# Eleven products of a decoder layer computed by token and turned by transposing DMAs

## The chip, the cores and the metric

The kernel runs on one core of a Trainium2 chip. The metric is the time of one execution on the device, in microseconds. A run executes the whole layer once. For a profile, one execution is recorded by the hardware profiler.

## The reference

A hybrid decoder layer for one sequence of 256 tokens, model width 2048, in float32. With `hn = rmsnorm(h)`:

```python
q, k, v, g_ret, xr, yr, g_a, g_b = split(hn @ w_in)      # widths 1024 1024 2048 2048 2048 2048 2048 2048
q, k   = rotary(q, positions), rotary(k, positions) * 128**-0.5
ret    = head_groupnorm(chunkwise_retention(q, k, v))    # 8 heads, chunks of 128 tokens
xr     = causal_dwconv(xr, rnn_conv_w, rnn_conv_b)       # 4 taps along the tokens
hr     = rg_lru(xr, ...)                                 # gates by 16 blocks of 128, scan along the tokens
merged = sigmoid(g_a) * ((silu(g_ret) * ret) @ w_proj_ret) + sigmoid(g_b) * ((gelu(yr) * hr) @ w_proj_rnn)
h      = h + merged @ w_mix_out
h      = h + memory_cross_attention(rmsnorm(h), rmsnorm(mem), ...)   # 256 memory tokens, 4 heads
h      = h + conv_gated_ffn(rmsnorm(h), ...)             # width 5632, conv of 3 taps
out    = rmsnorm(h)
```

The change touches `q`, `k`, `xr` and `yr`: they are the four parts of `hn @ w_in` that are used with features on the partitions (rotation across features, convolution and scan along tokens).

## The kernel before

**Products in two parts.** Every large product is made from float32 numbers split into a high and a low part (`hi` and `lo`, type float32r): high by high, high by low and low by high are summed. Weights come as pieces of 4 x 128 rows by 512 columns (1 MB). A planner's list, `weight_plan`, fixes their order, and `prefetch` keeps two pieces ahead (`AHEAD = 2`): a load on SP's queue into `raw` (six buffers), `hi` by a ScalarE copy (line 286), `lo` by a VectorE subtraction (line 287), three buffers each. One piece is one unit of the loop `units`. A paired product (`pair_products`) computes two column blocks with fewer multiplications; its eleven units are half or full ones, and two of them get their weights by a load that accumulates on GpSimd's queue, after a VectorE addition (line 294).

**Two forms of a product.** `gemm_n` gives rows: tokens on the partitions, 512 features in the free dimension; the activations are the stationary operand and the weights stream, 24 matmuls of 512 columns a unit (lines 362, 363, 369). `gemm_t` gives columns: features on the partitions, 256 tokens in the free dimension; the weights are stationary. It streams high and low activations together (512 columns) through each high weight block and the high activations (256 columns) through each low one, 16 and 16 matmuls a unit (line 351). Its result lies in two PSUM tiles, in halves that `joined` adds (a ScalarE copy, line 544, and a VectorE addition, line 545). `scaled` is `joined` and a multiplication by the token's reciprocal root mean square `rsb2` (line 676).

**A turn by DMA.** In the feed-forward part, all but three of the up products are already made by `gemm_n` and turned: `planes` copies the float32 rows as two planes of 16-bit words (line 757), `turn_planes` issues two transposing DMAs from SP's queue (line 1205), `join_planes` puts the words together again by two ScalarE copies for each pair of feature blocks (line 763), and a multiplication by `rsb2` follows (line 1271). The three that aren't so made use `gemm_t`, as do the first queries.

**The order of work.** The program is one straight line. `later(n, fn)` puts off a piece of work until n + 1 units have gone by. In it stand, among others, the retention (`retain`: scores, values, statistics, head stores), and the recurrence (`recur`: gates by TensorE at line 948, exponentials, scan). The scheduler orders each engine's instructions by the program's order and by what is ready, and fixes that order before the run; buffers come from pools (`big`: 24 of 4 KB a partition, `tmp`: 10 of 2 KB, three PSUM tiles `acc`).

For each of the two groups of four heads the kernel before computes queries by `gemm_t`, values by `gemm_n` or as a pair, keys by `gemm_t`, gates as a pair, and then the retention. `rotated` turns queries and keys by position (lines 720, 722, 726, and the split at 552 and 553). Then come four recurrent blocks; each makes `xr` and `yr` by `gemm_t`, with `scaled`, the convolution (lines 995 and 997) or the gelu (lines 1005 to 1009) right behind it.

Of the kernel before, what the change touches and what calls it, by code (L numbers as in the profile page):

```python
# [29 lines left out]
KC = 4  # L30
# [124 lines left out]
def hybrid_layer(  # L155
# [37 lines left out]
    def tmp(s="t"):  # L193
        return tp.tile([P, 2, S], F32, tag="tmp", name=nm(s))
# [109 lines left out]
    def later(n, fn):  # L304

        pending.append((step[0] + n + 1, fn))
# [403 lines left out]

    def rotated(qs_):

        o = []
        cb = cos[:, None, :].to_broadcast([P, 2, S])
        for pr in range(2):
            q = qs_[pr]
            ta, tb = tmp("ta"), tmp("tb")
            dve.tensor_tensor(out=ta, in0=q, in1=cb, op=ALU.mult)  # L720
            for lo_, hi_ in ((0, 64), (64, 128)):
                dve.tensor_tensor(  # L722
                    out=tb[lo_:hi_], in0=q[64 - lo_ : 128 - lo_],
                    in1=sin[64 - lo_ : 128 - lo_, None, :].to_broadcast([64, 2, S]), op=ALU.mult,
                )
            dve.tensor_add(ta, ta, tb)
            o.append(split_pair(ta))
        return o

    class Kept(list):  # L730
# [9 lines left out]
        def __getitem__(self, i):  # L740
# [9 lines left out]
    def words(t):  # L750

        return t.bitcast(U16).rearrange("p t (w two) -> p t w two", two=2)

    def planes(t, rows, cs=slice(0, BW)):

        for i in range(2):
            act.copy(t[:, :, i, cs], words(rows)[:, :, :, 1 - i])

    def join_planes(d, pr):

        t = tmp("jp")
        for i in range(2):
            ins = act.copy(words(t)[:, :, :, 1 - i], d[:, i, 2 * pr : 2 * pr + 2, :])  # L763
            if i == 0:
                tc.keep_in_program_order(ins)
        return t

    class KeptRows(list):
        def __init__(self, name, wcol=None):
# [112 lines left out]
    for g in range(2):  # L882
        dec = big([P, 4, S], s="dec")
        vs, turned = [], []
        for b, o in enumerate((O_Q, O_K)):
            a = qjoin if g == b == 0 else [joined(t, "q") for t in gemm_t("w_in", 0, xs, NT, o + g * BW)]
            if b == 0:
                sp.dma_start(
                    out=dec,
                    in_=consts[:, C_DEC + g * 4 * S : C_DEC + (g + 1) * 4 * S].rearrange("p (h s) -> p h s", s=S),  # L890
                )
            if g > 0:
                turned.append(rotated(a))
                if b == 0:
                    vs += [split_rows(v, rs0) for v in pair_out("w_in", xs, xs_sums, O_V + 1024)]
            else:
                if b == 1:
                    turned.append(rotated(a))
                v = gemm_n("w_in", 0, xs, NT, O_V + b * BW)
                if b == 0:  # L900
                    turned.append(rotated(a))
                    for i in range(KC):
                        later(i, lambda i=i: sum_x(i))
                vs.append(split_rows(v, rs0))
        qr, kr = turned
# [79 lines left out]
    def recurrent(b):  # L985
        rgw = big([P, 2, 4, P], s="rgw")
        for i, src in enumerate((rg_w_a, rg_w_x)):
            sp.dma_start(out=rgw[:, i], in_=src[0, 4 * b : 4 * b + 4].rearrange("g i j -> i g j"))
        xr = big([P, 4, S], s="xr")
        for pr, a in enumerate(gemm_t("w_in", 0, xs, NT, O_XR + b * BW)):  # L990
            z = scaled(a, "xz")
            for j in range(2):
                t = 4 * b + 2 * pr + j
                y = xr[:, 2 * pr + j, :]
                act.activation(y, z[:, j, :], AF.Identity, scale=p_cw(3, t), bias=p_cb(t))
                for s in range(1, 4):
                    dve.scalar_tensor_tensor(
                        out=y[:, s:S], in0=z[:, j, 0 : S - s], scalar=p_cw(3 - s, t), in1=y[:, s:S],
                        op0=ALU.mult, op1=ALU.add,
                    )  # L1000
        gl = big([P, 4, S], s="gl")
        for pr, a in enumerate(gemm_t("w_in", 0, xs, NT, O_YR + b * BW)):
            y = scaled(a, "yz")
            y2, th = tmp("y2"), tmp("yt")
            act.activation(y2, y, AF.Square)
            dve.tensor_scalar(out=y2, in0=y2, scalar1=0.044715 * K0, scalar2=K0, op0=ALU.mult, op1=ALU.add)
# [175 lines left out]

    qs = KeptRows("qs")

    def row_planes(o):

        t = big([P, 2, 2, BW], U16, s="rp")
        planes(t, o)
        return t

    for b in (0, 2):
        for i in range(KC):
            if b == 0 and i < 2:
# [7 lines left out]
    def turn_planes(rows):  # L1201

        d = big([P, 2, KC, S], U16, s="d")
        for tt in range(2):
            sp.dma_start_transpose(  # L1205
                out=d.rearrange("p a c s -> p (a c) s")[:, :, tt * P : (tt + 1) * P],
                in_=rows[:, tt].rearrange("p a w -> p (a w)"),
            )
        return d

    def turn_key(b, o):
        d = turn_planes(row_planes(o))
# [48 lines left out]
    def up(c0, b, at, then):  # L1261

        if at is None:
            for pr, a in enumerate(gemm_t("ffn_w_up", 0, h2s, NT, c0 + b * BW)):
                then(pr, scaled(a, "uz"))
            return
        d = turn_planes(row_planes(gemm_n("ffn_w_up", 0, h2s, NT, c0 + b * BW)))

        def turned(pr):
            z = join_planes(d, pr)  # L1270
            dve.tensor_tensor(out=z, in0=z, in1=rsb2, op=ALU.mult)
            then(pr, z)

        for pr in range(2):
            later(at[pr], lambda pr=pr: turned(pr))

    def conv(c0, b, pr, z, dst):
        for j in range(2):
# [84 lines left out]
    for part, nb_ in enumerate(FF_PARTS):  # L1363
# [3 lines left out]
        for b in range(b0, b0 + nb_):  # L1367
            gt, vl = big([P, 4, S], s="fg"), big([P, 4, S], s="fv")
            last = b + 1 == b0 + nb_
            up(0, b, (1, 2), lambda pr, z, b=b, gt=gt: conv(0, b, pr, z, gt))  # L1370
            if last:
                later(0, lambda part=part, n=2 if paired else 4: get_rows(part % 2, range(n)))

# [4 lines left out]
            if last and paired:  # L1378
                for pr, a in enumerate(gemm_t("ffn_w_up", 0, h2s, NT, FF + b * BW)):
                    later(1 + 2 * pr, lambda pr=pr, z=scaled(a, "uz"): finish_up(pr, z))  # L1380
            else:
                up(FF, b, None if last else (1, 2), finish_up)
        if final:
            wfin = []
            for i in range(2):
# [51 lines left out]
```

## Time and profile before

| | |
|---|---|
| median of 3 runs | 1984.11 us (1982.38 to 1986.17) |
| the profiled execution | 1986.44 us |
| its span | 1984.6 us, granted TensorE clock 0.998 |
| busy: TensorE, VectorE, ScalarE | 1968.9, 1568.1, 1271.2 us |
| data read and written in device memory | 420.96 MB and 16.78 MB |

The span runs from the first to the last recorded instruction; what the profiled execution has beyond it lies before and after. Busy times of an engine are the union of its instructions. In the lines below, PE is TensorE's matmul, PEld its weight load, DVE is VectorE, ACT ScalarE, POOL GpSimd, SP the sync engine; a "q" behind the name is the engine's instruction queue. `out<-in` are the program's names of the tiles. In a group the two numbers behind the bar are busy microseconds and the mean nanoseconds of one instruction, then the idle time of the engine just before them, with what ended it.

### The profile page before, as it was taken

The page shows a single profiled execution, that of the slowest core. Times are in us where ns is not written, and L with a number is a line of the kernel's source. Part 1 is how long each engine was busy: PE and PEld are TensorE (multiplying, and loading weights), DVE is VectorE, ACT ScalarE, POOL GpSimd, SP SyncE. Part 2 cuts the span into 40 slices and gives each one's busy share as a digit, 9 for nine tenths or more (in the row PEclk, how much of TensorE's full clock was granted, in tenths as well). Part 3 has the DMA queues.
Part 4 walks back from the last instruction along what each step waited for, and adds up shares of the span by engine and source line. Part 5 has one row for each costly group of instructions (what it writes and reads, how often), then busy time and mean ns, then how long its engine had stood idle before and what let it go on. Part 6 is the DMA issues. An engine that isn't in the chain of part 4 may idle for free.

```text
span 1984.6 us, 23752 instructions
## 1 busy us (share of the span) xinstructions
PE 1968.9 (99%) x9368; PEld 1653.5 (83%) x9368; DVE 1568.1 (79%) x1550; ACT 1271.2 (64%) x1315; POOL 43.2 (2%) x52
## 2 busy tenths in 40 slices
PE   9999999999999999999999999999999999999998
PEld 8888888888888888888888888888878888888887
DVE  6988887889986876778888868677797776985775
ACT  6555656768667654566878756567754676646663
POOL 0000000000000000000000000000000000000000
PEclk9999999999999999999999999999999999999999
DMA  9675674655887775778998838767778567786671
GB/s 365 235 256 149 234 260 164 217 205 143 274 256 220 254 254 179 249 264 241 287 249 231 288 113 233 266 222 221 214 239 284 196 224 239 224 279 232 212 245 63
DMA packets 142239, 455.54 MB, mean 230 GB/s; under 512 B 73520, under 2 KB 78256, under 8 KB 94384
## 3 DMA queue, kind: packets, MB, share of 16 engines
q1 hardware_dynamic: 134848, 409.46, 58.7%
q0 software_dynamic: 5760, 41.95, 11.6%
q10 hardware_dynamic: 1520, 2.63, 0.4%
q8 instruction: 73, 1.20, 0.2%
q14 instruction: 38, 0.31, 0.0%
HBM read 420.96 MB, written 16.78 MB: 221 GB/s over the span
## 4 chain that ended last, share of the span: by engine, by line
PE 90%; DVE 4%; issue 2%; DMA 2%; ACT 1%; SPq 0%; POOLq 0%; ACTq 0%; DVEq 0%
PE acc L369 24%; PE acc L362 24%; PE acc L363 24%; PE acc L351 15%; PE sm L518 2%; DVE lo L287 2%; DMA raw<-in_wall 2%; ACT hi L286 1%; PE acc L518 1%; PE sm L948 1%; PE sm L532 1%; DVE raw L294 0%; DVE fv L1283 0%; DVE tb L722 0%; SPq L1205 0%
## 5 line engine op out<-in xcount | busy, mean ns | idle before, releaser
L287 DVE TENSOR_TENSOR lo<-raw,hi 128x2048 fp32r<-128x2048 f32 (+1 forms) x420 | 951.1, 2268 | 283.9 <-ACT hi L286 279.5
L286 ACT CAST hi<-raw 128x2048 fp32r<-128x2048 f32 (+1 forms) x418 | 792.7, 1901 | 511.7 <-PE acc L363 353.7
L362 PE MATMUL acc<-hi,s 128*128 128x512 f32 x1944 | 760.1, 391 | 2.1 <-ACT s L555 2.1
L363 PE MATMUL acc<-hi,s 128*128 128x512 f32 x1944 | 758.0, 390 | 0.4 <-DVE s L556 0.4
L369 PE MATMUL acc<-lo,s 128*128 128x512 f32 x1944 | 485.2, 389 | 0.0
L362 PEld LDWEIGHTS acc<-hi,s 128*128 128x128 f32 x1944 | 365.5, 188 | 78.0 <-ACT s L555 3.3
L363 PEld LDWEIGHTS acc<-hi,s 128*128 128x128 f32 x1944 | 365.7, 188 | 76.2 <-DVE s L556 1.3
L369 PEld LDWEIGHTS acc<-lo,s 128*128 128x128 f32 x1944 | 364.9, 188 | 75.8
L351 PE MATMUL acc<-s,hi 128*128 128x512 f32 x960 | 232.1, 393 | 0.9 <-DVE hi L284 0.9
L351 PEld LDWEIGHTS acc<-s,hi 128*128 128x128 f32 x960 | 178.0, 189 | 36.8 <-issue 1.1
L351 PEld LDWEIGHTS acc<-s,lo 128*128 128x128 f32 x960 | 123.9, 192 | 5.2 <-DVE lo L287 1.1
L351 PE MATMUL acc<-s,lo 128*128 128x256 f32 x960 | 127.2, 284 | 0.5 <-DVE lo L287 0.5
L362 PE MATMUL acc<-hi,ss 128*128 128x512 f32 x320 | 125.8, 393 | 1.1 <-ACT o L454 0.6
L363 PE MATMUL acc<-hi,ss 128*128 128x512 f32 x320 | 124.7, 390 | 0.0
L763 ACT COPY jp<-d 128x512 uint16<-128x512 uint16 x124 | 87.9, 772 | 35.0 <-DMA d<-rp 34.8
L369 PE MATMUL acc<-lo,ss 128*128 128x512 f32 x320 | 85.6, 389 | 0.0
L362 PEld LDWEIGHTS acc<-hi,ss 128*128 128x128 f32 x320 | 60.1, 188 | 15.1 <-ACT o L454 1.5
L369 PEld LDWEIGHTS acc<-lo,ss 128*128 128x128 f32 x320 | 60.1, 188 | 12.6
L363 PEld LDWEIGHTS acc<-hi,ss 128*128 128x128 f32 x320 | 60.1, 188 | 12.1
L267 POOL DMA_DIRECT2D raw<-in_wall x40 | 35.2, 879 | 1543.5 <-DVE lo L287 1047.5
L427 DVE TENSOR_TENSOR nat<-nat,acc 128x512 f32<-128x512 f32 (+1 forms) x49 | 44.0, 910 | 6.0 <-PE acc L369 6.0
L292 DVE TENSOR_TENSOR raw<-raw,raw 128x2048 f32<-128x2048 f32 x20 | 45.8, 2289 | 0.4
(235 smaller groups left out, 1254.8 us busy)
## 6 DMA issues: line engine op xcount, KB each, us to landing
raw<-in_wall SPq DMA_DIRECT2D x333, 1024.0 KB, 5.1
raw<-in_wall POOLq DMA_DIRECT2D x40, 1024.0 KB, 8.2
fkept<-nat SPq DMA_DIRECT2D x12, 512.0 KB, 7.6
nat<-fkept SPq DMA_DIRECT2D x12, 512.0 KB, 4.6
xt<-in_x_t SPq DMA_DIRECT2D x11, 256.0 KB, 8.0
raw<-in_wall SPq DMA_DIRECT2D x5, 512.0 KB, 8.6
nat<-in_x ACTq DMA_DIRECT2D x4, 512.0 KB, 9.8
ret<-hr SPq DMA_DIRECT2D x4, 512.0 KB, 4.7
```

What stands on the lines that cost most here:

```text
L267: pool.dma_start(out=raw, in_=src, accum_op=ALU.add)
L286: act.copy(hi[:, a:b], raw[:, a:b])
L287: dve.tensor_tensor(out=lo[:, a:b], in0=raw[:, a:b], in1=hi[:, a:b].bitcast(F32), op=ALU.subtract)
L292: dve.tensor_tensor(out=to, in0=to, in1=by, op=ALU.add)
L351: pe.matmul(a, part, sx, start=k == 0 and t == 0, stop=k == nk - 1 and t == 0, skip_group_check=True)
L362: pe.matmul(o, h, hi, start=start and kk == 0, stop=False, skip_group_check=True)
L363: pe.matmul(o, l, hi, start=False, stop=False, skip_group_check=True)
L369: pe.matmul(o, h, lo, start=False, stop=stop and kk == KC - 1, skip_group_check=True)
L427: dve.tensor_tensor(out=o, in0=o, in1=i, op=op)
L518: ins = pe.matmul(o, a, b, start=start and i == 0, stop=stop and i == 2, skip_group_check=True)
L532: ins = pe.transpose(t[:, j, tt * P : (tt + 1) * P], rows[:, tt, k + j * P : k + (j + 1) * P], ident)
L763: ins = act.copy(words(t)[:, :, :, 1 - i], d[:, i, 2 * pr : 2 * pr + 2, :])
```

## The change

Eleven products go from `gemm_t` to `gemm_n` with the turn by DMA: keys of the first head group, queries and keys of the second, `xr` and `yr` of the four recurrent blocks. The first queries stay as they are. The helpers of the turn move up in the file, and `gemm_turned` puts them together: product, planes, transposes, and for each of the two pairs of feature blocks a join put off by `at` (and `at + 1`) units, with `then` behind it. `at` is 1 for the first keys and for the recurrent products, 3 where paired products follow. With `shared` (recurrent products) the second of the two plane copies is VectorE's. `by_rs` multiplies by `rsb2`. The feed-forward part uses the same helper with the delays that it had.

```diff
+    def planes(t, rows, cs=slice(0, BW), shared=False):
+        for i in range(2):
+            copy = dve.tensor_copy if i and shared else act.copy
+            copy(t[:, :, i, cs], words(rows)[:, :, :, 1 - i])
...
+    def gemm_turned(w, st, col, at, then, shared=False):
+        d = turn_planes(row_planes(gemm_n(w, 0, st, NT, col), shared))
+        for pr in range(2):
+            later(at + pr, lambda pr=pr: then(pr, join_planes(d, pr)))
+
+    def by_rs(z):
+        dve.tensor_tensor(out=z, in0=z, in1=rsb2, op=ALU.mult)
+        return z
...
-        for b, o in enumerate((O_Q, O_K)):
-            a = qjoin if g == b == 0 else [joined(t, "q") for t in gemm_t("w_in", 0, xs, NT, o + g * BW)]
...
+        def block(o, at, turned=turned):
+            halves_ = []
+            def then(pr, z):
+                halves_.append(z)
+                if pr == 1:
+                    turned.append(rotated(halves_))
+            gemm_turned("w_in", xs, o + g * BW, at, then)
+
+        if g == 0:
+            vs.append(split_rows(gemm_n("w_in", 0, xs, NT, O_V), rs0))
+            turned.append(rotated(qjoin))
+            for i in range(KC):
+                later(i, lambda i=i: sum_x(i))
+            block(O_K, 1)
+            vs.append(split_rows(gemm_n("w_in", 0, xs, NT, O_V + BW), rs0))
+        else:
+            block(O_Q, 3)
+            vs += [split_rows(v, rs0) for v in pair_out("w_in", xs, xs_sums, O_V + 1024)]
+            block(O_K, 3)
         gates = [head_gate(a, big([P, 2, BW], s="gate")) for a in pair_out("w_in", xs, xs_sums, O_G + g * 1024)]
-        retain(g, qr, kr, vs, dec, gates)
+        retain(g, *turned, vs, dec, gates)
...
-        for pr, a in enumerate(gemm_t("w_in", 0, xs, NT, O_XR + b * BW)):
-            z = scaled(a, "xz")
+        def conv_x(pr, z):
+            by_rs(z)
...
+        gemm_turned("w_in", xs, O_XR + b * BW, 1, conv_x, True)
...
-        for pr, a in enumerate(gemm_t("w_in", 0, xs, NT, O_YR + b * BW)):
-            y = scaled(a, "yz")
+        def gelu(pr, y):
+            by_rs(y)
...
+        gemm_turned("w_in", xs, O_YR + b * BW, 1, gelu, True)
         later(0, lambda: recur(b, rgw, xr, gl))
...
-        d = turn_planes(row_planes(gemm_n("ffn_w_up", 0, h2s, NT, c0 + b * BW)))
...
+        gemm_turned("ffn_w_up", h2s, c0 + b * BW, at, lambda pr, z: then(pr, by_rs(z)))
```

More of the change, by code (lines that the diff above doesn't have):

```diff
@@ L748, in __getitem__ @@
             return list.__getitem__(self, i)
[L750 to L766, printed above, removed]
     class KeptRows(list):
@@ L1183, in hybrid_layer @@
     qs = KeptRows("qs")
[L1185 to L1189, printed above, removed]
     for b in (0, 2):
@@ L1199, in hybrid_layer @@
             later(1 + 2 * i, lambda b=b + i, o=o: qs.store(b, row_planes(o)))
[L1201 to L1209, printed above, removed]
     def turn_key(b, o):
@@ L1381, in hybrid_layer @@
             else:
-                up(FF, b, None if last else (1, 2), finish_up)
+                up(FF, b, None if last else 1, finish_up)
         if final:
```

52 lines of the change are left out of this document (26 added, 26 removed).

## The prediction

> **What bounds the kernel now.** I read the page's busy shares first, then TensorE's own waits (engine, tile and line, who it waited for: us in all, times, longest), then the chain of work in order of time, and last the timeline and the windows of the stages that the change touches.
>
> ```profile
> span 1984.6 us, 23752 instructions
> PE 1968.9 (99%) x9368; PEld 1653.5 (83%) x9368; DVE 1568.1 (79%) x1550; ACT 1271.2 (64%) x1315; POOL 43.2 (2%) x52
> ...
> PE acc L362 <- ACT s L555: 2.1, 3, 1.5
> ...
> PE acc L362 <- ACT o L454: 0.6, 2, 0.3
> ...
> PE acc L362 <- DVE o L470: 0.5, 1, 0.5
> ```
>
> TensorE is idle for 1984.6 - 1968.9 = 15.7 us in all. The three waits shown are 3.2 us of it; the last two, 1.1 us together, lie in the paired products of values and gates of the second head group, a part that the change touches. So only TensorE's own work, or new idle time on it, can move the end. VectorE and ScalarE matter only where they come too late for TensorE.
>
> ```profile
> 345.74 38.94 PE acc L351 x224
> 386.41 5.55 PE acc L351 x32
> 393.70 38.94 PE acc L351 x224
> 434.37 5.55 PE acc L351 x32
> ...
> 1281.01 1.81 PE acc L369 x8
> 1286.45 1.81 PE acc L369 x8
> ...
> 1378.93 1.81 PE acc L369 x8
> ```
>
> This is the chain in order of time (start, length, what). Line 351 is the product by feature (`gemm_t`); 224 matmuls are seven weight units of 32, so a unit costs 38.94 / 7 = 5.563 us. Lines 362, 363 and 369 are the product by token (`gemm_n`), 24 matmuls a unit; the closing group of eight recurs every (1378.93 - 1281.01) / 18 = 5.440 us. Both stretches run without a gap.
>
> ```profile
> 450.70 4.00 PE L351 MATMUL acc<-s,lo 128*128 128x256 f32 x32
> 454.53 7.44 PE L351 MATMUL acc<-s,hi 128*128 128x512 f32 x32
> 461.81 3.04 PE L351 MATMUL acc<-s,lo 128*128 128x256 f32 x24
> ```
>
> The timeline of TensorE says why the two differ though both stream 12,288 columns a unit. From start to start, 32 matmuls of 256 columns take 3.83 us (0.1197 each) and 32 of 512 take 7.28 us (0.2275 each). The narrow one costs more than half of the wide one. `gemm_t` has 16 of each a unit, 5.555 us; `gemm_n` has 24 wide ones.
>
> **The change part by part.** Eleven products of four units each (keys of the first head group, queries and keys of the second, four recurrent inputs, four recurrent gates) go from `gemm_t` to `gemm_n`. All of it is on the path: 44 x (5.563 - 5.440) = 5.4 us less of TensorE. No other TensorE instruction is added or removed, since the turn is made by DMA.
>
> Around it the other engines' work changes:
>
> ```profile
> L763 ACT COPY jp<-d 128x512 uint16<-128x512 uint16 x124 | 87.9, 772 | 35.0 <-DMA d<-rp 34.8 <-DMA d<-ret 0.2
> ...
> L757 ACT COPY rp<-acc 128x1024 uint16<-128x1024 uint16 x38 | 36.3, 1007 | 0.0
> ...
> L460 DVE TENSOR_TENSOR o<-o,acc 128x1024 f32<-128x1024 f32 x22 | 26.8, 1218 | 10.5 <-PE acc L369 10.4
> ...
> L544 ACT COPY c<-acc 128x512 f32<-128x512 f32 x30 | 17.2, 579 | 11.5 <-PE acc L351 11.1
> ...
> L722 DVE TENSOR_TENSOR tb<-q,sin 64x512 f32<-64x512 f32 x16 | 11.0, 686 | 0.3
> ...
> L545 DVE TENSOR_TENSOR xz<-acc,c 128x512 f32<-128x512 f32 x8 | 5.4, 679 | 0.0
> ...
> L1006 DVE TENSOR_SCALAR y<-y 128x512 f32<-128x512 f32 x8 | 3.4, 422 | 1.4 <-ACT y L1005 1.4
> ```
>
> These are groups by line and shape (mean ns behind the comma). Each product loses two ScalarE copies of half sums (2 x 0.579) and two VectorE additions (2 x 0.679). It gains two plane copies out of PSUM and four joining copies (4 x 0.772 = 3.09 us, ScalarE). For keys and queries both plane copies are ScalarE's (2 x 1.007): +3.94 us for ScalarE, -1.36 for VectorE. For the eight recurrent products one plane is VectorE's: +2.94 us for ScalarE. VectorE's price for that copy isn't in the trace. Below it lies twice the one-source 512-element row, 0.84 us; above it the 1024-element addition that also reads PSUM, 1.22 us. I take 1.22, since it shares the PSUM source: -0.14 us for VectorE a product. The multiplication by the token scale stays, now at its own place in a shared helper.
>
> The Trainium skill (VectorE: DVE Perf Modes, "The perf-mode tier table" and "Mode 2×_1P") says that a PSUM operand leaves at most the packed double rate and that this needs 16-bit elements at step one; the copy reads every second 16-bit word, so it would run at one element a cycle, an estimate of (120 + 1024) / 0.96 = 1.19 us by that page's cycle table. The sum would be the same; no run here shows it yet.
>
> ```profile
> core 0: us, PE busy (x) PEld busy (x) DVE busy (x) ACT busy (x) POOL busy (x), PEclk, DMA share, GB/s
> 338.46:386.41 47.95, 47.95 (x274) 42.39 (x273) 40.67 (x48) 37.21 (x49) 0.00 (x0) 1.00 0.69 241
> 386.41:434.37 47.96, 47.96 (x274) 42.40 (x273) 39.71 (x46) 32.16 (x40) 0.00 (x0) 1.00 0.55 198
> 469.30:516.80 47.50, 47.50 (x213) 39.48 (x212) 45.58 (x37) 40.31 (x45) 1.75 (x2) 1.00 0.74 217
> 1281.00:1379.00 98.00, 98.00 (x435) 81.12 (x434) 73.52 (x90) 68.82 (x73) 0.00 (x0) 1.00 0.67 214
> ```
>
> In these windows the first two are recurrent blocks (the first still stores heads), the third the paired gate product behind the last block, the fourth the feed-forward part, which already works as the change wants it. A recurrent block loses 8 x 0.123 = 1.0 us on TensorE, so it lasts 47.0. ScalarE goes from 32.16 to 32.16 + 2 x 2.94 = 38.0 us (81%), with head stores 43.1 (92%); VectorE stays at 39.4 (84%). The feed-forward window shows planes, transposes and joins at 70 to 75% load with TensorE at 98.00 of 98.00. So inside the blocks I cost the added work at nothing: the cover is the two units that the casts run ahead, about 11 us.
>
> ```profile
> SPq L265 <- DVE lo L287: 1131.2, 259, 16.9
> ...
> SPq L1205 <- ACT rp L757: 56.1, 14, 5.9
> ...
> ACT hi L286 <- PE acc L351: 43.1, 30, 4.7
> ACT jp L763 <- DMA d<-rp: 34.8, 15, 4.8
> ...
> d<-rp SPq DMA_TRANSPOSE x46, 3.3
> ```
>
> The 22 new transposes go through SP's queue. Behind an SP instruction that waits for the planes (5.9 us at worst so far) stand the weight loads, and behind them the casts. Those loads wait for free buffers anyhow, 1131.2 us in total, and six raw buffers of 5.4 us hold more than 30 us: nothing. A join on ScalarE waits for its transpose (34.8 us in 15 cases, 4.8 the longest); queued behind it are weight casts. ScalarE's waits for TensorE to free a cast buffer (43.1 us by line 351) say that the casts run as far ahead as buffers allow. `gemm_n` also uses the low weights last in a unit, where `gemm_t` has them first in every second one. Nothing, with the price of this cover in the rivals.
>
> Two places have less cover, because paired products have units of half length. Behind the last block:
>
> ```profile
> 487.68 1.92 ACT L286 CAST hi<-raw 128x2048 fp32r<-128x2048 f32 x1
> 489.61 1.28 ACT L963 ACT_TABLE_LOAD   x1
> 490.91 1.06 ACT L963 ACTIVATE tt<-tt 128x1024 f32<-128x1024 f32 x1
> 492.04 1.07 ACT L454 COPY o<-acc 128x512 f32<-128x512 f32 x2
> 493.00 5.55 ACT L286 CAST hi<-raw 128x2048 fp32r<-128x2048 f32 x3
> ...
> 495.39 4.49 DVE L287 TENSOR_TENSOR lo<-raw,hi 128x2048 fp32r<-128x2048 f32 x2
> ...
> 497.28 0.39 PE L362 MATMUL acc<-hi,s 128*128 128x512 f32 x1
> ...
> 500.90 1.98 PE L369 MATMUL acc<-lo,s 128*128 128x512 f32 x8
> ```
>
> ScalarE is full here. The first of three casts ends at 494.9, and TensorE wants it at 497.28: 2.4 us of cover. The last recurrent gates add 1.0 + 3.1 - 0.6 (one of the two half-sum copies already fell before) = 3.5 us ahead of it. So TensorE would wait 1.1 us; VectorE's low cast (4.49 / 2 = 2.25 us, begun at 495.39) isn't wanted until 500.90. I charge +1.1; the bounds are 0 (the scheduler moves the cast ahead) and 3.5 (no cover).
>
> The other place is the second head group's queries and keys. Their joins and the rotation move from the start of a paired product to its fourth and fifth unit. A rotation is ten VectorE operations of about 0.69 us, 6.9 us, and now stands before the short units; its old place becomes free, and the addition that starts the accumulating load comes earlier. Bounds: -1.1 us (the two old waits go) to +6.9 us each (no cover). Casts two units ahead and a 5.4 us unit right behind the short ones lie nearer to the lower end: 0.
>
> Sum: -5.4 + 1.1 = -4.3 us. Against the profiled execution (span 1984.6, time 1986.44, 1.84 outside the span) that is a span of 1980.3. The median of runs, 1984.11, is 2.3 below the profiled time; with the same -4.3 it becomes 1979.8. About 0.2%, 4.0 us, is what a measurement of this kernel can tell from no change, so the forecast lies just beyond it.
>
> **The rivals.**
>
> *Given back in part.* Each of the three paired products costs 1.1 to 1.8 us as in the sum, because every one gets planes and joins: 5.4 - 3 x 1.5 = 0.9 us remain, 1983.2. For it: ScalarE at 40.31 of 47.50 and VectorE at 45.58 in the third window. Against it: casts ahead elsewhere.
>
> *The narrow matmul was not the cost.* If 256 columns cost just their share, nothing is gained but a fixed piece per matmul. With 0.1137 (half of 0.2275) a unit of `gemm_t` would be 16 x 0.3412 = 5.46 us, and 44 x 0.02 = 0.9 us would be left: 1983.2. Against it: 5.563 and 5.440 come from long gapless stretches of this trace. The Trainium skill (VectorE: DVE Perf Modes, "The TRN2 errata") gives a matmul max(60, 6 + columns) cycles of 2.4 GHz, an estimate of 5.20 and 5.18 us for the two units, thus 0.9 us over the 44. The trace disagrees: 0.1197 us where that rule gives 0.109.
>
> *Slower: the rotation lands before the short units.* Three short units need three low casts and one weight addition from VectorE, 4 x 2.3 = 9.2 us in 3 x 2.72 = 8.2; with 6.9 more it is 7.9 behind, against 5.4 us of casts ahead. From 2.7 us of idle TensorE a place, at two places, the gain is gone. With the whole rotation uncovered it is 2 x 6.9 - 5.4 = +8.4 us: 1992.5; with half, +1.5. For it: VectorE's 96% in a paired product. Against: rotation and low casts have different readiness, and the order can be filled.
>
> **How the numbers follow.** Forecast 0.65, of which 0.10 ends less than 4.0 us below; given back 0.13; narrow matmul not the cost 0.05; slower 0.17. Faster by over 0.2%: 0.55. Within: 0.10 + 0.13 + 0.05 = 0.28. Slower: 0.17. The low end takes the whole 5.4 and both old waits, 1.1, off: 1977.6, less 0.8 for the scatter of a median, 1976.8. The high end takes in the slower rival up to a quarter of its uncovered case beyond the break-even, about +3.4: 1987.5.
>
> **What would show it.** Line 351 of TensorE should fall from 960 + 960 matmuls to 256 + 256, the `gemm_n` lines rise by 352 each. Recurrent blocks should recur every 47.0 us where it was 47.95, with units of 5.44. Transposes go from 46 to 68, joining copies from 124 to 168; ScalarE's busy time grows by 3 x 3.94 + 8 x 2.94 = 35 us, VectorE's falls by about 5. New TensorE waits should be some 1 us, near 500 us, for a cast. I am wrong if TensorE's busy time falls by other than 5 us, or if its idle time grows by more than 3 us; then the rows of TensorE's waits name the place.

## The result: slower by 0.7%, and the profile after

| | before | after |
|---|---|---|
| median | 1984.36 us (4 runs, 1982.38 to 1986.17) | 1999.03 us (4 runs, 1995.79 to 1999.60) |
| ratio, with its 95% interval | | 1.007 (1.0058 to 1.0082) |
| profiled execution, its span | 1986.44, 1984.6 us | 1999.6, 1997.8 us |
| TensorE busy, idle | 1968.9, 15.7 us | 1971.4, 26.4 us |

The forecast was 1979.8 us, 4.3 below; the change costs 14.7 us instead. TensorE still bounds the kernel, but both parts of its time moved the wrong way: 10.7 us more idle, and 2.5 us more busy where 5.4 less was expected.

The page after: engines first, then three groups (line, engine, tiles, shape and count; busy us, mean ns; idle time before them).

```profile
PE 1971.4 (99%) x9016; PEld 1638.0 (82%) x9016; DVE 1564.9 (78%) x1536; ACT 1298.2 (65%) x1351; POOL 44.8 (2%) x52
...
L727 ACT COPY jp<-d 128x512 uint16<-128x512 uint16 x168 | 118.6, 770 | 65.2 <-DMA d<-rp 63.8
...
L351 PE MATMUL acc<-s,hi 128*128 128x512 f32 x256 | 63.8, 397 | 1.3 <-DVE hi L284 1.3
...
L721 ACT COPY rp<-acc 128x1024 uint16<-128x1024 uint16 x52 | 50.1, 1006 | 0.0
```

The change does what it says: 256 wide matmuls are left in `gemm_t`, joins went from 124 to 168. The row to stop at is the first group: ScalarE now stands 63.8 us at a join for a transposing DMA, where it stood 34.8. TensorE's own waits after (us in all, times, longest) say that some of that reached the end:

```profile
PE acc L362 <- ACT s L555: 4.0, 3, 1.9
PE acc L369 <- DVE lo L287: 3.4, 3, 3.1
PE sm L980 <- ACT ti L983: 2.4, 2, 2.2
PE acc L362 <- DVE v L568: 2.1, 1, 2.1
```

The second and fourth lie at one place, the third at another; the first is in code that the change left alone.

**Place 1: behind the first keys.** The timeline after, all engines (start, length, engine, what; in brackets the idle time before it and what ended it):

```profile
82.82 0.91 ACT L899 ACTIVATE xt<-xt,pa 128x256 f32<-128x256 f32 x2 [1.96 <-DMA xt<-in_x_t]
...
86.20 1.91 ACT L721 COPY rp<-acc 128x1024 uint16<-128x1024 uint16 x2
...
88.14 2.71 SPq L742 DMA_TRANSPOSE d<-rp  x2
88.45 1.04 POOL L267 DMA_DIRECT2D raw<-in_wall  x1 [49.17 <-DVE lo L287]
...
99.69 2.67 ACT L727 COPY jp<-d 128x512 uint16<-128x512 uint16 x4 [8.47 <-DMA d<-rp]
```

and TensorE's alone, behind it:

```profile
109.55 2.08 PE L369 MATMUL acc<-lo,ss 128*128 128x512 f32 x4 [3.09 <-DVE lo L287]
...
113.67 0.79 PE L362 MATMUL acc<-hi,s 128*128 128x512 f32 x1 [2.05 <-DVE v L568]
114.27 0.63 PE L363 MATMUL acc<-hi,s 128*128 128x512 f32 x1
114.69 0.63 PE L362 MATMUL acc<-hi,s 128*128 128x512 f32 x1
```

Read it downwards. The plane copies of the keys come at 86.20, behind the sums over x (line 899) in ScalarE's written order, and those wait for a load. The two transposes go out at 88.14 and 89.54; between them, 0.3 us after the first and 1.1 us before the second, GpSimd's queue issues the 1 MB load that accumulates. The transposes land 7.2 and 10.1 us after their issue. ScalarE stands at the pinned join for 8.47 us, with the next weight cast behind it; the rotation and the low casts come late on VectorE; TensorE waits 3.1 and 2.1 us. Then it runs slow: the starts at 113.67 and 114.27 lie 0.60 us apart, and from 114.27 on a start follows every 0.43 us where it was 0.227. Windows of the same 39 matmuls, after and before (window, its length, busy us and count of TensorE, its weight loads, VectorE, ScalarE and GpSimd, mean granted clock, DMA share, GB/s):

```profile
104.00:122.00 18.00, 12.85 (x39) 9.44 (x38) 16.24 (x13) 9.99 (x10) 0.87 (x1) 0.72 0.27 72
```

```profile
105.00:113.50 8.50, 8.50 (x39) 7.06 (x38) 6.76 (x3) 5.08 (x3) 0.87 (x1) 1.00 0.40 131
```

9.5 us are lost here: 5.2 of waiting, 4.3 of slower matmuls; the granted clock of the window is 0.72 on the mean, where it was 1.00. The Trainium skill (TensorE: Matmul & The Clock Gate, "Part 1: The HAM clock gate") says that the array falls to half its clock when a free-running window of about 3.4 us finds it idle, and needs such a window to come back. The trace agrees in kind: 0.43 against 0.227 us, for about 6 us. It differs in length: no wait here reached 3.4 us, and spells of 3.1 and 2.1 us (of 2.2 at place 2) were enough.

**Place 2: gates of the third recurrent block.** The same view, later:

```profile
438.08 1.89 PE L980 MATMUL sm<-xr,rgw 128*128 128x256 f32 x8
...
440.68 1.40 ACT L727 COPY jp<-d 128x512 uint16<-128x512 uint16 x2 [2.30 <-DMA d<-rp]
...
443.39 0.84 ACT L982 ACTIVATE tr<-sm,h 128x256 f32<-128x256 f32 x2
...
445.97 0.63 ACT L1044 ACTIVATE yt<-y 128x512 f32<-128x512 f32 x1 [1.22 <-DVE y L1043]
...
447.12 0.46 ACT L983 ACTIVATE ti<-sm,h 128x256 f32<-128x256 f32 x1
...
447.63 3.58 PE L980 MATMUL sm<-xr,rgw 128*128 128x256 f32 x8 [2.21 <-ACT ti L983]
```

The first half of the gates' products was ready at about 440. ScalarE, which reads them out of PSUM (`tr`, then `ti`), first stood at a join of the gelu branch for its transpose (2.3 us), then at the gelu's tanh for VectorE (1.2 us). The second half of the gates' products needs the PSUM tile that `ti` frees: TensorE waits 2.2 us. By the starts of the same instructions before and after, 3.4 us are lost between 432 and 479.

**Balance.** Measured by such starts, after is 0.9 us ahead at 105, 8.1 behind at 174, 5.6 behind at 432 (the recurrent blocks give 2.5 back), 9.0 at 479, 9.5 at 522 and at 1030, 13.0 at the end. So a third term of 3.5 us arises after 1030 us, 2.8 of it idle time of TensorE, where no instruction is changed and the order on ScalarE, VectorE, GpSimd and SP is that of before.

### The profile page after: what moved, and what is told of

Same layout as the page of the kernel before. It is cut to its first block, busy times and chain, and to the rows that moved or that the text cites. A ratio compares the mean times of both kernels' runs of the same rounds, so it can differ in the third digit from the quotient of the medians.

```text
span 1997.8 us, 23107 instructions
## 1 busy us (share of the span) xinstructions
PE 1971.4 (99%) x9016; PEld 1638.0 (82%) x9016; DVE 1564.9 (78%) x1536; ACT 1298.2 (65%) x1351; POOL 44.8 (2%) x52
## 4 chain that ended last, share of the span: by engine, by line
PE 86%; DVE 5%; DMA 3%; ACT 3%; issue 2%; SPq 1%; POOLq 0%; ACTq 0%; DVEq 0%
PE acc L362 27%; PE acc L363 27%; PE acc L369 26%; PE acc L351 2%; DVE lo L287 2%; PE sm L518 2%; DMA raw<-in_wall 2%; DMA d<-rp 1%; ACT hi L286 1%; PE acc L518 1%; SPq L742 1%; PE sm L980 1%; PE sm L532 1%; ACT jp L727 0%; DVE tb L767 0%
## 5 line engine op out<-in xcount | busy, mean ns | idle before, releaser
L362 PE MATMUL acc<-hi,s 128*128 128x512 f32 x2296 | 900.5, 392 | 6.0 <-ACT s L555 4.0
L363 PE MATMUL acc<-hi,s 128*128 128x512 f32 x2296 | 897.0, 391 | 0.5 <-DVE s L556 0.5
L369 PE MATMUL acc<-lo,s 128*128 128x512 f32 x2296 | 572.9, 389 | 0.2 <-DVE lo L287 0.2
L362 PEld LDWEIGHTS acc<-hi,s 128*128 128x128 f32 x2296 | 432.8, 189 | 97.6 <-ACT s L555 5.2
L363 PEld LDWEIGHTS acc<-hi,s 128*128 128x128 f32 x2296 | 432.6, 188 | 90.1 <-DVE s L556 1.3
L369 PEld LDWEIGHTS acc<-lo,s 128*128 128x128 f32 x2296 | 430.8, 188 | 90.1 <-DVE lo L287 0.6
L727 ACT COPY jp<-d 128x512 uint16<-128x512 uint16 x168 | 118.6, 770 | 65.2 <-DMA d<-rp 63.8
L755 DVE TENSOR_TENSOR jp<-jp,rsb 128x512 f32<-128x512 f32 x54 | 36.8, 689 | 38.4 <-ACT jp L727 38.4
L351 PE MATMUL acc<-s,hi 128*128 128x512 f32 x256 | 63.8, 397 | 1.3 <-DVE hi L284 1.3
L351 PEld LDWEIGHTS acc<-s,hi 128*128 128x128 f32 x256 | 48.2, 192 | 10.9 <-issue 1.5
L721 ACT COPY rp<-acc 128x1024 uint16<-128x1024 uint16 x52 | 50.1, 1006 | 0.0
## 6 DMA issues: line engine op xcount, KB each, us to landing
nat<-in_x ACTq DMA_DIRECT2D x4, 512.0 KB, 10.7
```

What stands on the lines that cost most here:

```text
L351: pe.matmul(a, part, sx, start=k == 0 and t == 0, stop=k == nk - 1 and t == 0, skip_group_check=True)
L362: pe.matmul(o, h, hi, start=start and kk == 0, stop=False, skip_group_check=True)
L363: pe.matmul(o, l, hi, start=False, stop=False, skip_group_check=True)
L369: pe.matmul(o, h, lo, start=False, stop=stop and kk == KC - 1, skip_group_check=True)
```

## The experiments

Twenty kernels in one table; the ratio is to the kernel before, run beside each on the same chip (its medians were 1983.69 to 1985.14). The last column is the row "ACT jp <- DMA d<-rp" of ScalarE's waits after 1000 us, in unchanged code, in the one profiled execution of each kernel; that one can lie at the edge of its runs (e3's took 1991.88 us, e6's 1989.50, e13's 1988.83, e16's 1982.08). The edit has one more difference, which stays in every kernel but the one before: in the second head group the load of the decays is issued ahead of the queries' product and no longer behind it. No run takes that back by itself.

| kernel | products by token | median us | ratio | joins wait |
|---|---|---|---|---|
| before | 0 | | 1 | 34.8 |
| e4, second head group alone | 2 | 1982.91 | 0.9996 | 35.4 |
| e16, e10 without the second group's keys | 5 | 1984.37 | 1.0001 | 38.6 |
| e10, e4 and recurrent inputs | 6 | 1981.07 | 0.9985 | 30.7 |
| e15, e13 without the second group's keys | 6 | 1981.08 | 0.9985 | 36.1 |
| e18, e10 with two more DMAs | 6 | 1981.26 | 0.9987 | 36.2 |
| e11, e4 and recurrent gates | 6 | 1992.76 | 1.0043 | 35.8 |
| e13, e10 and first keys, sums early | 7 | 1984.52 | 1.0003 | 43.3 |
| e17, e13 with two more DMAs | 7 | 1984.38 | 1.0004 | 40.5 |
| e20, e13 with two more large buffers | 7 | 1986.76 | 1.0011 | 41.1 |
| e21, e13 with two more small buffers | 7 | 1985.48 | 0.9998 | 41.0 |
| e3, all recurrent products alone | 8 | 1986.63 | 1.0014 | 33.4 |
| e9b, all but the last block, sums early | 9 | 1987.40 | 1.0017 | 40.1 |
| e1, all but the first keys | 10 | 1986.25 | 1.0011 | 35.7 |
| e5, e1 with both planes on ScalarE | 10 | 1988.46 | 1.0020 | 33.2 |
| e6, e1 with joins a unit later | 10 | 1993.16 | 1.0046 | 37.7 |
| e7, e1 with both | 10 | 1986.52 | 1.0007 | 38.8 |
| after | 11 | 1999.03 | 1.0070 | 43.7 |
| e2, after with the first keys' joins later | 11 | 1999.02 | 1.0076 | 43.3 |
| e8, after with the sums early | 11 | 1989.52 | 1.0026 | 42.7 |

### First keys: e1, e2, e8, e3

e1 takes them back; e2 only puts their joins off; e8 moves the sums over x ahead of the first values, so that they no longer stand before the planes; e3 takes back everything but the recurrent products.

```diff
 e1
-            block(O_K, 1)
+            turned.append(rotated([joined(t, "q") for t in gemm_t("w_in", 0, xs, NT, O_K)]))
 e2
-            block(O_K, 1)
+            block(O_K, 3)
 e8
+            for i in range(KC):
+                later(i, lambda i=i: sum_x(i))
             vs.append(split_rows(gemm_n("w_in", 0, xs, NT, O_V), rs0))
             turned.append(rotated(qjoin))
-            for i in range(KC):
-                later(i, lambda i=i: sum_x(i))
 e3
 e1, and for both products of the second head group:
-            block(O_Q, 3)
+            turned.append(rotated([joined(t, "q") for t in gemm_t("w_in", 0, xs, NT, O_Q + BW)]))
```

> The changed kernel with one edit: the first head group's keys are again made by feature, without planes, transposes and joins. Theory A (a held queue: ScalarE stands at a pinned join whose transposes are late, and the weight casts behind it come too late): of the 18.6 us that the change loses beside its gain of 5.4, 9.5 lie at this one place (3.1 + 2.1 us of idle TensorE and some 4 us of a lowered clock behind it). They go, and 0.5 us of the gain with them: 1999.0 - 9.0 = 1990.0 us. Theory B (load: the 35 us of added ScalarE work push casts back all over the changed part): only the 3.9 us of this product's added work go, a ninth: about 1997.4. Theory C (the 3.7 us that appear after 600 us are caused by the change too): no statement on this run's sum, but then that part stays.

> The changed kernel with one edit: the first keys' joins are put off by 3 and 4 units instead of 1 and 2. Theory A, with the order of ScalarE's instructions as the scheduler leaves it (the first join still stands before the same number of weight casts but one, because the scheduler pulls it forward as soon as it reckons the transposes done): the queue is held as before, 1997 to 1999.5 us. Theory A without that (the delay as written counts): the join comes some 11 us later, when the transposes have landed, 1990. Theory B (load): the same work at another place, no change, 1999.

> The changed kernel with one edit: the four sums of the activations (loads, scaling and splits, sum_x) are put into the four units of the first values instead of the four units of the first keys. Nothing is added or left out. Theory A: the plane copies of the first keys no longer stand on ScalarE behind a load for the last sum (they began 11.5 us after the product's end), the transposes are issued some 8 to 10 us earlier and ahead of the accumulating weight load, and the join doesn't wait: 1999.0 - 9.4 = 1989.6 us, 0.5 better than with the keys back. Theory B (load): the same load, 1998 to 1999.5. A third way: the sums now collide with the position tables and the value product; then idle TensorE before 55 us, up to 5 us.

> Only the eight recurrent products by token; all keys and queries by feature as before the change. Theory A: gain 8 x 4 x 0.123 = 3.9 us, loss at one place (the third block's gates wait for a PSUM tile that ScalarE frees late: 2.2 us idle and 1.7 us of slower matmuls), so 1984.4 - 3.9 + 3.9 = 1984.4 us, and if the 3.7 us after 600 us come with this part, 1988. Theory B (load, shared out by the added ScalarE work, 23.5 of 35.3 us): 1984.4 - 3.9 + 12.4 = 1992.9.

e1: 1986.25, so 12.8 of the 14.7 us hang on one product of eleven (ratio to before 1.0011, 1.0003 to 1.0020). The 12.8 are two losses: e8 gets 9.5 back with these keys still by token, about what place 1 lost, and the other 3.3 are the loss in unchanged code, which comes last. e2: 1999.02, no change: in the written order the joins stayed where they were and ran at 99.1 us, after a wait of 8.3. e8: 1989.52. Its timeline shows why:

```profile
83.44 1.92 ACT L721 COPY rp<-acc 128x1024 uint16<-128x1024 uint16 x2
...
85.38 2.71 SPq L742 DMA_TRANSPOSE d<-rp  x2
...
89.83 1.04 POOL L267 DMA_DIRECT2D raw<-in_wall  x1 [50.98 <-DMA d<-rp]
90.01 2.66 ACT L727 COPY jp<-d 128x512 uint16<-128x512 uint16 x4 [2.85 <-DMA d<-rp]
```

The planes come 2.8 us earlier, the accumulating load goes out behind the transposes, and these land in 3.3 us instead of up to 10.1. Place 1 is gone, TensorE runs through it. The Trainium skill (Trainium Kernel Development and Optimization, "Key Constraints") says that DMAs from the SP, ScalarE and GpSimd queues share the same 16 engines and interleave; both traces agree with that, but no run had the load alone moved, so how much of the 10.1 us it makes stays open. In e2 the load again goes out 0.3 us behind the first transpose, and they land in 7.1 and 10.0 us. e3: 1986.63, the recurrent products lose by themselves.

### Recurrent products: e5, e6, e7, with e4

On the base of e1: e5 gives both planes to ScalarE, e6 puts the joins off by a unit, e7 does both; e4 leaves the recurrent products out altogether.

```diff
 e5
-        gemm_turned("w_in", xs, O_XR + b * BW, 1, conv_x, True)
+        gemm_turned("w_in", xs, O_XR + b * BW, 1, conv_x, False)
 e6
+        gemm_turned("w_in", xs, O_XR + b * BW, 2, conv_x, True)
 e7
+        gemm_turned("w_in", xs, O_XR + b * BW, 2, conv_x, False)
 (the same for O_YR and gelu)
 e4
+        for pr, a in enumerate(gemm_t("w_in", 0, xs, NT, O_XR + b * BW)):
+            conv_x(pr, joined(a, "xz"))
+        for pr, a in enumerate(gemm_t("w_in", 0, xs, NT, O_YR + b * BW)):
+            gelu(pr, joined(a, "yz"))
```

> First keys back by feature, and both plane copies of the eight recurrent products on ScalarE (VectorE's late copy goes). Base of comparison: the kernel with only the first keys back, 1986.25. Theory A (the rest is lost where the gates of the third recurrent block stand behind a late join; the join is late because the transposes wait for VectorE's plane): about 3.4 us come back, 1982.9. Theory B (the loss is the gelu steps standing between the gates' ScalarE steps, whichever engine makes the plane): the order of ScalarE keeps such a step in the third block, so 1 to 2 us at most, 1984.5 to 1985.5. Theory C (ScalarE is simply too full; eight more copies of 1.0 us make it worse): above 1987.

> First keys back by feature, joins of the recurrent products one unit later (VectorE's plane copy stays). Theory A (late joins): a transpose has 5.4 us more, 1982.9 if nothing else is late. Theory B (gelu steps between the gates' steps): in the third block all four gates' ScalarE steps now stand together, also 1982.9; so with the first kernel of this call A and B are told apart: A both, B only this one. Theory C (load of ScalarE): unchanged, 1986.2. Against all: behind the last block the last joins and gelu come a unit later, beside the short units, +1 at most.

> First keys back, joins one unit later and both planes on ScalarE. Theory A and B: 1982.5 (the 3.4 us of the third block and some of the 0.5 at the paired gates come back). Theory C: above 1987.

> Only the queries and keys of the second head group by token; first keys and recurrent products as before. By the sum of the prediction: 2 x 4 x 0.123 = 1.0 us of TensorE and up to 1.1 us of two old waits less, 1981.6 to 1982.7 where the kernel before has 1983.7. The rival of the prediction (rotation before the short units) expects +1.5 to +8.4 less 1.0, above 1984.2.

e4: 1982.91 (0.9996, 0.9987 to 1.0004), a little above the band expected: the second head group shows no cost beyond its gain, and the interval holds both no change and what its eight units promise. The three others missed: none came to 1982.9. In e5 the third block is clean, but the fourth has the same wait, larger:

```profile
469.50 5.20 SPq L742 DMA_TRANSPOSE d<-rp  x2
...
476.80 1.40 ACT L727 COPY jp<-d 128x512 uint16<-128x512 uint16 x2 [5.35 <-DMA d<-rp]
...
489.03 0.47 ACT L983 ACTIVATE ti<-sm,h 128x256 f32<-128x256 f32 x1
...
489.55 2.07 PE L980 MATMUL sm<-xr,rgw 128*128 128x256 f32 x4 [5.28 <-ACT ti L983]
```

In e7, too, the third block is clean (4.5 us ahead of before at 479), and 5.3 us are lost from there to 562, with two waits for `ti` of 1.4 and 0.6 us at the fourth block's gates. In e6 there are five such waits, 3.0 us, and 3.1 us more for PSUM copies and a cast beside the short units. So neither VectorE's late plane nor the distance of the joins is the cause by itself; they move the wait from block to block.

### What stands ahead of `ti`: e10, e11, e13, e9b

The written order of ScalarE shows where the wait can be. Third or fourth block, from the first join to the end of the gates (J join, where copies stand together one letter; Y and T gelu, r, i, a, t the gates' four steps, C weight cast, s half sum, - table load). The kernel before has no join here, and its row starts at the table load:

```
before, block 3     -TsYCTriatriatCriatriat
e1, block 3         J-rrYTJiatiatJriaYtriaTt
e5, block 4         JCY-rrCTJCiatiatYriatriaTt
e10, block 3        YC-TsCYriatriaTtCriatriat
e11, blocks 3, 4    J-rYrCTJCiatiatYriatTriat   J-rrYCTJCiatiatYriatriaTt
```

Where J, Y, T or C stands between r and i, the PSUM tile stays taken until those are done. In e10 only the recurrent inputs are by token, in e11 only the gates; e13 is e10 with the first keys by token and the sums early; e9b is all of the change but the last block, both planes on ScalarE.

```diff
 e10 (on e1)
-        gemm_turned("w_in", xs, O_YR + b * BW, 1, gelu, True)
+        for pr, a in enumerate(gemm_t("w_in", 0, xs, NT, O_YR + b * BW)):
+            gelu(pr, joined(a, "yz"))
 e11 (on e1)
-        gemm_turned("w_in", xs, O_XR + b * BW, 1, conv_x, True)
+        for pr, a in enumerate(gemm_t("w_in", 0, xs, NT, O_XR + b * BW)):
+            conv_x(pr, joined(a, "xz"))
 e13 (on e8): the edit of e10
 e9b (on e8)
+        if b == 3:
+            ... as before
+        else:
+            gemm_turned("w_in", xs, O_XR + b * BW, 1, conv_x, False)
```

> First keys back, and only the four recurrent inputs by token (the recurrent gates by feature, as before); second head group by token. Theory O (what costs is a join or a gelu step that waits and stands, in the written order of ScalarE, ahead of the steps that read the gates' products; without gelu's joins the order of all four blocks is that of the kernel before): no TensorE wait for ti above 0.5 us, and 16 units x 0.123 = 2.0 us less than the kernel that has the second head group alone (1982.91): 1980.9. Theory L (ScalarE's added load costs, product by product): half of what the eight products cost (1986.25 to 1988.46 against 1982.91, so 3.3 to 5.6), 1984.6 to 1985.7.

> The other half: the recurrent gates by token, the inputs by feature. Theory O: the written order has a join or a gelu step between the gates' first and second steps in blocks 1, 3 and 4; two waits for ti of 2 us or more with slow matmuls behind them, 3 us each, less 2.0: 1986 to 1989 . Theory L: 1984.6 to 1985.7, the same as for the inputs.

> Recurrent inputs, first keys and second head group by token, recurrent gates by feature, and the sums over x moved into the units of the first values, so that the first keys' planes are not queued behind them. Theory O: 0.5 us less than with the first keys by feature: 1980.4, and faster than the kernel before. Theory L: 1984 to 1985.

> All of the change but the last recurrent block (by feature), both planes on ScalarE, and the sums moved as in the kernel before this one. Written order: in block 1 a join stands between the gates' steps (no wait was seen there so far), in 2 and 3 the gates' steps stand together, the last as in the kernel before. Theory O: 24 x 0.123 = 3.0 us, 1.5 for the second head group, 0.5 for the first keys: 1979.4. Theory L: three quarters of the recurrent loss: 1985 to 1987.

e10: 1981.07 (0.9985, 0.9976 to 0.9994), as theory O said, and no wait for `ti` is left in its list. e11: 1992.76; TensorE's waits in it begin with

```profile
PE sm L980 <- ACT ti L983: 6.2, 2, 3.4
PE acc L369 <- DVE lo L287: 2.3, 1, 2.3
```

Both halves add the same number of products and 14.4 to 16.2 us of ScalarE's busy time over before; they lie 11.7 us apart. So the total load is not the cause; the traces show the order at work, at the two waits for `ti`. Not all of the 11.7 us is that: e11's other wait, 2.3 us for `lo`, comes at 261 us, ahead of the recurrent blocks, in the paired gates of the second head group, where e10 waits 0.9 in the same instructions. With the slow matmuls behind them e11 is some 3 us further behind there. (So e11's loss was larger than either theory had.) The Trainium skill (Perfetto Trace Analysis, "Tensor Engine Instruction (MATMUL, LD_WEIGHTS)") says that ScalarE and VectorE work their queues strictly in order; all these rows agree, none shows a later step passing a waiting join.

e13 and e9b missed, by 4 and 8 us. In e9b a part is the same mechanism on VectorE. Its timeline, at the last block, which is by feature again:

```profile
449.32 1.28 DVE L992 SCALAR_TENSOR_TENSOR tt<-a,tt 128x512 f32<-128x512 f32 x2
...
450.52 1.28 DVE L545 TENSOR_TENSOR xz<-acc,c 128x512 f32<-128x512 f32 x2
...
451.26 2.03 PE L351 MATMUL acc<-s,hi 128*128 128x512 f32 x5 [3.19 <-DVE xz L545]
```

The addition that frees a PSUM tile stands behind the delayed gelu and recurrence of the block before. A second wait of e9b, 2.0 us for `lo` at 260 us, is that of e11 in the second head group. e13 has neither: its profiled execution is 3.3 us ahead of before up to 1030 us, and ends 2.2 behind.

### A loss in unchanged code: e15 to e18, e20, e21

The last column of the table goes with this loss. With the first keys by token (after, e2, e8, e13, e9b) the joins after 1000 us wait 40 to 44 us, without them 31 to 39. ScalarE's waits in e10 and in e13, after 1000 us:

```profile
ACT jp L727 <- DMA d<-rp: 30.7, 15, 4.8
```

```profile
ACT jp L727 <- DMA d<-rp: 43.3, 18, 6.9
```

TensorE's wait there, in e10 and in e13, is for `s`, an operand that ScalarE writes at line 555:

```profile
PE acc L362 <- ACT s L555: 0.8, 2, 0.5
```

```profile
PE acc L362 <- ACT s L555: 3.9, 2, 2.0
```

The timeline of e13 shows how the one becomes the other:

```profile
1459.46 1.90 ACT L286 CAST hi<-raw 128x2048 fp32r<-128x2048 f32 x1 [5.03 <-DMA raw<-in_wall]
...
1461.26 0.62 ACT L555 ACTIVATE s<-fo 128x512 fp32r<-128x512 f32 x1
```

The longest wait of a join (6.9 us, near 1420 us; 4.8 in e10) holds up VectorE's multiplication behind it. From there VectorE runs some 2 us later against TensorE than in e10. So does an accumulating weight load, which needs VectorE's addition first (issued at 1451.24 us, landed at 1459.36); its cast waits 5.03 us (3.23 in e10), and behind that cast stands `s`.

In the five kernels with the first keys by token the number of products by token is odd, in the others even. e15 and e16 change the number by the second group's keys; e17 and e18 add two DMAs and no buffers.

```diff
 e15 (on e13), e16 (on e10)
-            block(O_K, 3)
+            turned.append(rotated([joined(t, "q") for t in gemm_t("w_in", 0, xs, NT, O_K + BW)]))
 e17 (on e13), e18 (on e10): dec in two halves
+        for hh in range(2):
+            c0_ = C_DEC + (2 * g + hh) * 2 * S
+            sp.dma_start(out=dec[:, 2 * hh : 2 * hh + 2, :], in_=consts[:, c0_ : c0_ + 2 * S]...)
```

> The kernel with recurrent inputs, first keys (sums early) and second head group by token, but the keys of the second group back by feature: 12 added transposes in place of 14; 4 units x 0.123 = 0.5 us more of TensorE. Theory N (the later transposes land later when the number added before them is 2 above a multiple of 4): 1984.5 + 0.5 - 3.4 = 1981.6, joins after 1000 us wait 31 to 37 us. Theory K (the first keys by token do it in themselves): 1985.0, joins wait 40 to 44 us.

> The kernel with recurrent inputs and second head group by token and the first keys by feature, with the keys of the second group back by feature too: 10 added transposes in place of 12. Theory N: 1981.1 + 0.5 + 3.4 = 1985.0, joins after 1000 us wait 40 to 44 us. Theory K: 1981.6, 31 to 37 us.

> The kernel with 14 added transposes, the load of the decays split in two halves for each head group: two DMAs more on SP's queue, the same buffers, no other change. Theory N by the count of DMAs: 1981.1, joins after 1000 us wait 31 to 37 us. Theory N by the count of buffers taken, and theory K: 1984.5, 40 to 44 us.

> The kernel with 12 added transposes (first keys by feature), the load of the decays split in the same way. Theory N by the count of DMAs: 1981.1 + 3.4 = 1984.5, joins after 1000 us wait 40 to 44 us. By the count of buffers, and theory K: 1981.1, 31 to 37 us.

e15 1981.08, e16 1984.37: the loss goes with the number, by 3.3 to 3.4 us in the median, with or without the first keys. e17 1984.38, e18 1981.26: the count of DMAs does not. (The joins' waits of e16, 38.6, and of e7, 38.8, lie close together. TensorE's wait for `s` after 1000 us separates all twenty profiles: 3.7 to 4.0 us with an odd number, 0.8 to 3.1 with an even one, 2.1 in before.) A product by token takes two buffers more from the large ring of 24 and two fewer from the small ring of 10. e20 and e21 take two more of one kind, in e13:

```diff
             block(O_K, 1)
+            for _ in range(2):
+                dve.memset(big([P, 4, S], s="pad")[:, 0, 0:1], 0.0)      # e21: tmp("pad")
```

> The kernel with seven products by token (recurrent inputs, first keys with the sums early, second head group; 1984.5), with two more buffers taken from the large ring after the first keys' product and one word a partition written in each; nothing else. If the phase of the large ring sets the later landing: 1981.1, joins after 1000 us wait 31 to 39 us. If it is the small ring: 1984.5, 40 to 44 us.

> The same kernel with two more buffers taken from the small ring in the same place instead. Large ring: 1984.5, joins wait 40 to 44 us. Small ring: 1981.1, 31 to 39 us.

1986.76 and 1985.48, joins wait 41.1 and 41.0 us: two more buffers of either ring alone don't take the loss back. What it is about an odd number that makes later transposes land later stays open; both rings at once, and the ring of three PSUM tiles, were not tried.

## Why the prediction was wrong, point by point

**TensorE's gain: right.** By starts of the same gate products before and in e8, a block lasts 384.53 - 336.57 = 47.96 before:

```profile
336.57 1.89 PE L948 MATMUL sm<-xr,rgw 128*128 128x256 f32 x8
...
384.53 1.67 PE L948 MATMUL sm<-xr,rgw 128*128 128x256 f32 x7
```

and 380.26 - 333.15 = 47.11 in e8, where 47.0 was forecast (the next block takes 47.70 there, with a wait of 0.2 us for `ti` in it; in e5 both take 47.00):

```profile
333.15 1.89 PE L980 MATMUL sm<-xr,rgw 128*128 128x256 f32 x8
...
380.26 1.89 PE L980 MATMUL sm<-xr,rgw 128*128 128x256 f32 x8
```

So "the narrow matmul was not the cost" is refuted. e10 turns six products and gains 3.3 us in the median, by its sum 6 x 4 x 0.123 = 3.0.

**The step that failed: the joins "costed at nothing".** The prediction named what is queued behind a waiting join, weight casts, and found two units of cover for them. In the recurrent blocks it held for the casts; at the first keys it did not, a low cast came 3.1 us late. And other work stands behind a join: the gates' steps, on whose PSUM tile TensorE waits with no two units of cover. In after this costs 3.4 us at the third block; in the medians the gates by token cost 1986.25 - 1981.07 = 5.2 us where they should have gained 2.0. The feed-forward window that was taken as proof has no TensorE product waiting for ScalarE behind a join.

**The planes "at nothing".** The sum counted their length (1.0 us each) and SP's queue, not what stands before them on ScalarE. For the first keys that was the sums over x. The landing was seen at its median of 3.3 us; here it was 7.2 and 10.1. Place 1: 9.5 us, priced at 0, though the price of this cover had been promised to the rivals.

**A multiplier that the sum did not have.** The idle spells of some 2 us or more have slow matmuls behind them: 4.3 of the 9.5 us at place 1, 1.2 of the 3.4 at place 2. That is most of why TensorE's busy time rose by 2.5 us where it should have fallen by 5.4.

**The place near 497 us, +1.1.** No wait for a cast came there in after; from 479 to 522 it lost 0.5. The variants show that the place is dangerous, mostly for the gates' tile (5.3 us in e5); e6 alone also waits for a cast, 1.7 us at 538 us.

**The second head group, 0: right as far as e4 tells.** Its median is 1982.91, and the slower rival, a rotation before the short units, wanted more than 1984.2. In its trace one old wait is gone (0.6 us, line 454), but that for `o` of line 470 grew from 0.5 to 1.5 us and one of 0.8 us for a low part is new: 1.2 us more of waiting in all. "Given back in part" put its losses into the paired products; the second head group's gates (2.3 us in e11, 2.0 in e9b, 0.2 in after) and the fourth block's gates, which run beside a paired product, bear it out in some variants.

**Small terms.** VectorE's plane copy was taken at the upper bound, 1.22 us; it measured 1.22 (the estimate of 1.19 by the Trainium skill, VectorE: DVE Perf Modes, "The TRN2 errata", was 0.03 low). ScalarE's busy time grew by 27.0 us where 35 was forecast, VectorE's fell by 3.2 where it was about 5.

**Not in the sum at all:** the 3.3 us in unchanged code with an odd number of products. Why they arise stays open.

Put together from the medians: 1984.4 before; second head group 1982.9; with the recurrent inputs 1981.1; with the recurrent gates 1986.3; with the first keys 1999.0. The best kernels found, e10, e15 and e18, beat both: 0.9985 (0.9976 to 0.9994) for e10.

## What to carry to other kernels

When a step with a wait goes into an in-order engine, list everything that stands behind it up to the next tile that the bounding engine needs back, not just the obvious casts; the written order of that engine shows it before anything runs. A moved transfer is priced by what runs beside it at its new place. Idle time of TensorE cost 1.4 to 1.8 times its length here where it came in spells of 2 us or more (3.4 us lost for 2.2, 9.5 for 5.2, 7.3 for 5.3 in e5). A gain of 0.2% is no larger than the loss that an edit can cause far away, in code that it leaves alone, so build the halves of a change by themselves.

## What the runs showed of the hardware

Two transposes of the same size land in 3.3 us or less, or in 7.2 and 10.1 where a 1 MB accumulating load is issued between them (0.3 us behind the first, 1.1 ahead of the second). TensorE ran wide matmuls at 0.43 us instead of 0.227 for about 6 us after waits of 3.1 and 2.1 us. And in code that had not changed, TensorE's wait for one operand was 3.7 to 4.0 us where five, seven, nine or eleven products before it had been turned, and 0.8 to 3.1 where it was an even number or none: 3.3 us of the whole in the medians, by a mechanism that is still open.
